# A NaN-skipping row maximum on one core: some write-backs of tile 1 and tile 5 are given to VectorE

## The chip, the cores and the metric

The kernel runs on one core of a Trainium2 chip. The core's engines have their own instruction streams and wait for each other through semaphores: VectorE (DVE in the profile), ScalarE (ACT), GpSimd (POOL), TensorE (PE, unused here) and SyncE (SP), which issues the transfers. The metric is the device time of one launch in microseconds (us).

## What is computed

```python
def setup_inputs():
    batch, seq, dim = 32, 2048, 2048
    x = np.random.randn(batch, seq, dim).astype(np.float32)
    mask = np.random.rand(batch, seq, dim) < 0.1
    x[mask] = np.nan
    return {"x": x, "axis": -1}

def reference(x: np.ndarray, axis: int) -> np.ndarray:
    return np.nanmax(x, axis=axis).astype(np.float32)
```

Each of 65,536 rows of 2,048 numbers is reduced to its largest number that is not NaN. The input has 512 MiB, the output 256 KiB.

## The kernel before

The rows are dealt out over 128 partitions, 512 rows to each. The unit of the program is the **quarter row**: 512 elements per partition. The table `TILES` lists 74 tiles, and each entry has three lists in quarter rows: how the tile is loaded, in which pieces it is worked on, and in which parts it is reduced. The first tile has 4 quarter rows, all others 28 (7 rows per partition). Up to the 58th tile nearly all read `([28], [7, 9, 12], [16, 12])`: one load, three pieces, two reductions. Every eighth one (tiles 9, 17, 25, 33, 41) reads `([28], [9, 12, -7], [8, 20])`. From tile 59 on the pieces and then also the loads get smaller, up to 17 pieces and 19 loads in the last.

The work on a tile:

1. SP issues its loads into one of three buffers `xt` (line 245). A load waits for the last reduction of the tile that had the buffer before, three tiles ago.
2. ACT makes the **keys** of a piece (lines 419 to 427): from the upper 16 bits of each float it computes, with a Prelu of two slopes, a 16-bit number in one of three buffers `kt` of 12 quarter rows. For an ordinary number the key only mirrors these bits; for a NaN the slope sends it to a value that stands for minus infinity.
3. The **write-back** turns the keys round again (times -1, plus `TOP`) and puts them over the upper halves of the floats in `xt`, every second 16-bit word. By the sign of the piece in the table it is POOL (a positive number, `tensor_scalar`, line 279) or ACT (a negative one, `activation` with Copy, lines 392 to 404). A floating number regulates when it is issued: a negative one is held back until the next piece's keys, a positive one is joined to the piece ahead.
4. DVE takes the maximum along the rows (`tensor_reduce`, line 286).

At the end a row that held only NaNs is marked, and the results are stored.

Each engine executes its instructions in the order in which this loop issues them. The class `Order` puts one semaphore wait on each for what it needs: a key for its load and for a free key buffer, a write-back for its key, a reduction for the write-backs under it. The last piece of a tile that opens a new key buffer also waits until the next key buffer is free (lines 416 to 418); in the tiles of 7, 9 and 12 that buffer is the first piece's own, so that the third key of a tile waits for the first write-back of the same tile. `joints` finds pairs of a POOL and an ACT write-back that one reduction needs together, and `last` keeps for each key buffer the last event of each writer. The lines of the profile are those of this file; almost all of ACT's instructions have line 269, POOL's 279 and DVE's 286, which are the helpers that record them.

Of the kernel before, what the change touches and what calls it, by code (L numbers as in the profile page):

```python
# [10 lines left out]
Q = D // 4  # L11
# [2 lines left out]


TILES = (
    [([4], [4], [4])]
    + [([28], [7, 9, 12], [16, 12])] * 7
    + [([28], [9, 12, -7], [8, 20])]
    + [([28], [7, 9, 12], [16, 12])] * 7  # L20
    + [([28], [9, 12, -7], [8, 20])]
# [50 lines left out]
TOP = 0x7F7F  # L72
# [6 lines left out]


def total(pieces):
    return sum(sum(map(abs, p)) if isinstance(p, tuple) else abs(p) for p in pieces)


def with_last(c):

    return isinstance(c, float) and c > 0


def joints(pieces, reds):  # L90

    flat = []
    at = 0
    for step, parts in enumerate(pieces):
        for c in parts if isinstance(parts, tuple) else (parts,):  # L100

            if with_last(c):
                flat[-1] = (flat[-1][0], at + abs(c), False, step)
            else:
                flat.append((at, at + abs(c), c < 0, step + isinstance(c, float)))
            at += abs(c)
    needs = []
    done = 0
    for n in reds:
        over = [i for i, (a, b, _, _) in enumerate(flat) if a < done + n and b > done]  # L110
        done += n
        pools = [i for i in over if not flat[i][2]]
        backs = [i for i in over if flat[i][2]]
        if pools and backs and flat[pools[-1]][3] > flat[backs[-1]][3]:
            backs = []
        needs.append(pools[-1:] + backs[-1:])
    pairs = {}
    for need in needs:
        if len(need) == 2 and all(sum(i in n for n in needs) == 1 for i in need):
            for i in need:  # L120
                pairs[i] = tuple(need)
    return pairs
# [61 lines left out]
def kernel(  # L184
# [15 lines left out]
    nc = tc.nc  # L200
    P = nc.NUM_PARTITIONS
    f32, i32 = mybir.dt.float32, mybir.dt.int32
    i16, u16 = mybir.dt.int16, mybir.dt.uint16
    ALU = mybir.AluOpType
    ACT = mybir.ActivationFunctionType
# [34 lines left out]
    def load(out, source, deps):  # L240
        nonlocal turn
        e = order.add(
            "sp",
            nc.sync,
            lambda: nc.sync.dma_start(out=out, in_=source),  # L245
            deps + lanes[turn],
            lane=f"load{turn}",
            step=16,
        )
        lanes[turn] = [e]  # L250
        turn = (turn + 1) % LANES
        return e
# [12 lines left out]
    def act(deps, pair=None, **kw):  # L265
        return order.add(
            "act",
            nc.scalar,
            lambda: nc.scalar.activation(**kw),  # L269
            deps,  # L270
            lane=pair,
            joint=pair is not None,
        )

    def pool(deps, pair=None, **kw):
        return order.add(
            "pool",
            nc.gpsimd,
            lambda: nc.gpsimd.tensor_scalar(**kw),  # L279
            deps,  # L280
            lane=pair,
            joint=pair is not None,
        )

    def dve(deps, do, **kw):
        return order.add("dve", nc.vector, lambda: do(**kw), deps)  # L286
# [36 lines left out]
    clock = 0  # L323

    def last(uses):

        return list({back: e for back, _, e in sorted(uses, key=lambda u: u[1])}.values())

    key = 0
# [6 lines left out]
    for gi, (s, g) in enumerate(zip(rows, GROUPS)):  # L336
# [8 lines left out]
        for loads, pieces, reds in g:  # L345
            assert sum(loads) == total(pieces) == sum(reds)
            xt, before = xts[number % BUFS], free[number % BUFS]
            number += 1
            landed = []
            at = 0  # L350
            for c in loads:
                c *= Q
                if ahead:
                    e = ahead.pop(0)
                else:
                    e = load(xt[:, at : at + c], xg[:, base + at : base + at + c], before)
# [4 lines left out]
            at = done = 0  # L361
# [7 lines left out]
            flat = [c for c in each if not with_last(c)]  # L369
# [3 lines left out]
            piece = 0  # L373

            def cleaned(a, b, k, i, e):

                nonlocal clock
                clock += 1
                both = [(a, b, k, flat[i] < 0, clock)]
                if i in pairs:  # L380
                    if pairs[i] not in half:
                        half[pairs[i]] = both
                        return
                    both += half.pop(pairs[i])
                for a, b, k, back, when in both:
                    kfree[k].append((back, when, e))
                    clean.append((a, b, e))
# [17 lines left out]

            for parts in pieces:
                parts = parts if isinstance(parts, tuple) else (parts,)
                c = int(sum(map(abs, parts))) * Q
                here = [l for a, b, l in landed if a < at + c and b > at]
                kold = []  # L410
                if used + c > KEYS:
                    key = (key + 1) % NKEYS
                    used = 0
                    kold, kfree[key] = last(kfree[key]), []
                    assert all(k != key for q in half.values() for _, _, k, _, _ in q)
                    if at + c == sum(loads) * Q and number not in ALONE:

                        kold = kold + last(kfree[(key + 1) % NKEYS])
                e_key = act(
                    here + kold,  # L420
                    out=kts[key][:, used : used + c],
                    in_=xt[:, at : at + c].bitcast(i16)[:, 1::2],
                    func=ACT.Prelu,
                    bias=EDGE,
                    scale=-1.0,
                    alpha=float(TOP - LOW) / (EDGE - NAN),
                )
                release()
                for c in parts:
                    on = more.pop(0)  # L430
                    back, wait, c = c < 0, isinstance(c, float), int(abs(c)) * Q
                    kp = kts[key][:, used : used + c]
                    used += c
                    at += c
                    if back:
                        held.append((at - c, at, key, kp, e_key, piece))
                        if not wait or at == sum(loads) * Q:
                            release()
                    else:
                        group.append((at - c, used - c, key))  # L440
                        if not on:
                            assert all(k == key for _, _, k in group)
                            lo, klo, _ = group[0]
                            e = pool(
                                [e_key],
                                name(piece),
                                out=xt[:, lo:at].bitcast(i16)[:, 1::2],
                                in0=kts[key][:, klo:used],
                                scalar1=-1.0,
                                scalar2=float(TOP),  # L450
                                op0=ALU.mult,
                                op1=ALU.add,
                            )
                            group = []
                            cleaned(lo, at, key, piece, e)
                    piece += not on
                    open_ = [h[0] for h in held + group] + [p[0] for q in half.values() for p in q]
                    while reds and done + reds[0] <= min([at] + open_):
                        n = reds.pop(0)


                        lo = done - 1 if done % D else done
                        done += n
                        row = (base + lo) // D
                        if done % D:
                            m, to = 1, xt[:, done - 1 : done].bitcast(f32)
                        else:
                            m = max(n // D, 1)
                            to = acc[:, row : row + m]
                        e = dve(  # L470
                            [e for a, b, e in clean if b > lo and a < done] + part,
                            nc.vector.tensor_reduce,
                            out=to,
                            in_=xt[:, lo:done]
                            .bitcast(f32)
                            .rearrange("p (c d) -> p c d", c=m),
                            axis=mybir.AxisListType.X,
                            op=ALU.max,
                        )
                        part = [e] if done % D else []  # L480
                        after.append(e)
# [10 lines left out]
        else:  # L492
            e = find(after, maxima(lo, flagged))
            ready += [e] * (gi + 1 - len(ready))
        if gi == len(GROUPS) - 1:
            e = find_late(late_after, late_acc, late)
            ready[LATE] = e
    for (og, bits), e in zip(stores, ready):
# [6 lines left out]
            step=16,  # L505
# [38 lines left out]
```

## Time and profile before

| | before |
|---|---|
| time, median of 3 runs (lowest to highest) | 1250.2 us (1250.16 to 1250.34) |
| time of the profiled execution | 1250.19 us |
| its span | 1248.9 us |
| DVE busy, instructions | 1110.2 us, 183 |
| ACT busy, instructions | 974.4 us, 290 |
| POOL busy, instructions | 1162.3 us, 243 |
| read from memory | 536.87 MB, 430 GB/s over the span |

The profile is of one execution, and its span is 1.3 us shorter than that execution's time. A group's row gives the line, the engine, the operation, output and input with their shapes and the count, then the time it was busy, the mean of one in ns, and the engine's idle time just before these instructions with what ended it. A timeline's row gives start and length in us (of several instructions in a run, with their count), and in brackets the idle time ahead and what released it. A row of the windows gives the stretch, its length, the busy time of DVE, ACT and POOL with counts, the granted TensorE clock, and the share and rate of the transfers.

### The profile page before, as it was taken

Reading aid. Unit: us, or ns where it says so; the run is one execution under the profiler, and the core shown is the slowest. Engines: PE = TensorE matmul, PEld = TensorE weight load, DVE = VectorE, ACT = ScalarE, POOL = GpSimd, SP = SyncE. Lnnn points to the kernel's source line nnn. Section 1 sums busy time; section 2 is a strip of 40 time slices with the busy share of each in tenths; the row PEclk is TensorE's granted clock in tenths of the full one; section 3 lists DMA queues with packets and bytes.
Section 4 is the critical chain, followed back from the end, with each engine's and each line's share of the span. In section 5 each row is a group of like instructions: output and inputs, shape, how many; then the busy total and the mean of one; then the engine's idle time right before and its main releaser. Section 6 shows DMA issues by size and latency. Waiting matters only on the chain.

```text
span 1248.9 us, 918 instructions
## 1 busy us (share of the span) xinstructions
DVE 1110.2 (89%) x183; ACT 974.4 (78%) x290; POOL 1162.3 (93%) x243
## 2 busy tenths in 40 slices
DVE  0888989888889888898988888988888998999999
ACT  3777887778777877788777877777777789989998
POOL 2999989998999899998999899999999989999898
DMA  9999999999999999999999999999999999999998
GB/s 416 439 415 439 441 441 426 426 441 441 433 419 441 441 433 421 439 441 439 430 424 441 439 435 419 441 441 433 422 437 441 437 434 419 437 428 431 433 426 327
DMA packets 17720, 537.21 MB, mean 430 GB/s; under 512 B 2736, under 2 KB 2736, under 8 KB 5552
## 3 DMA queue, kind: packets, MB, share of 16 engines
q1 hardware_dynamic: 17712, 537.14, 99.6%
q14 instruction: 8, 0.07, 0.0%
HBM read 536.87 MB, written 0.26 MB: 430 GB/s over the span
## 4 chain that ended last, share of the span: by engine, by line
DVE 37%; DMA 36%; POOL 16%; ACT 9%; issue 2%; SPq 0%
DMA xt<-in_x_dram 36%; DVE acc L286 23%; POOL xt L279 16%; DVE lead L286 14%; ACT kt L269 8%; ACT xt L269 1%; SPq L245 0%; SPq L263 0%; SPq L254 0%
## 5 line engine op out<-in xcount | busy, mean ns | idle before, releaser
L279 POOL TENSOR_SCALAR xt<-kt 128x6144 int16<-128x6144 uint16 (+9 forms) x237 | 1161.1, 4899 | 83.2 <-ACT kt L269 69.4
L269 ACT ACTIVATE kt<-xt 128x6144 uint16<-128x6144 int16 (+11 forms) x256 | 914.1, 3610 | 266.3 <-DMA xt<-in_x_dram 245.6
L286 DVE TENSOR_REDUCE acc<-xt 128x3 f32<-128x6144 f32 (+4 forms) x123 | 896.3, 7329 | 129.8 <-POOL xt L279 122.5
L286 DVE TENSOR_REDUCE lead<-xt 128x1 f32<-128x2048 f32 (+3 forms) x57 | 213.2, 3812 | 4.0 <-POOL xt L279 3.9
L269 ACT ACTIVATE xt<-kt 128x512 int16<-128x512 uint16 (+4 forms) x32 | 61.8, 1932 | 0.7
L269 ACT ACT_TABLE_LOAD x1 | 1.3, 1283 | 3.3 <-PEq L263 3.3
L318 DVE MEMSET lead<- 128x1 f32 x1 | 0.1, 59 | 3.4 <-PEq L263 3.4
L279 POOL TENSOR_SCALAR lead<-lead 128x91 int32<-128x91 f32 x1 | 0.6, 552 | 0.1
L286 DVE SCALAR_TENSOR_TENSOR acc<-acc 128x414 f32<-128x414 f32 x1 | 0.6, 592 | 0.0
L314 POOL TENSOR_TENSOR lead<-lead 128x91 int32<-128x91 int32 x1 | 0.4, 377 | 0.1
L525 POOL MEMSET const-float32-0.0<- 128x1 f32 x1 | 0.1, 99 | 0.2 <-issue 0.2
L269 ACT ACTIVATE lead<-lead 128x1 f32<-128x1 f32 x1 | 0.2, 203 | 0.0
L286 DVE SCALAR_TENSOR_TENSOR lead<-lead 128x7 f32<-128x7 f32 x1 | 0.2, 167 | 0.0
L525 POOL MEMSET const-bfloat16-1.0<- 128x1 bf16 x1 | 0.1, 102 | 0.0
L525 POOL MEMSET const-uint8-127<- 128x1 uint8 x1 | 0.1, 102 | 0.0
L525 POOL MEMSET const-float32-1.0<- 128x1 f32 x1 | 0.1, 99 | 0.0
## 6 DMA issues: line engine op xcount, KB each, us to landing
xt<-in_x_dram SPq DMA_DIRECT2D x61, 7168.0 KB, 22.6
xt<-in_x_dram SPq DMA_DIRECT2D x3, 4096.0 KB, 18.1
xt<-in_x_dram SPq DMA_DIRECT2D x5, 2048.0 KB, 30.6
xt<-in_x_dram SPq DMA_DIRECT2D x3, 3072.0 KB, 25.0
xt<-in_x_dram SPq DMA_DIRECT2D x8, 1024.0 KB, 29.1
xt<-in_x_dram SPq DMA_DIRECT2D x3, 2560.0 KB, 22.4
xt<-in_x_dram SPq DMA_DIRECT2D x2, 3584.0 KB, 23.3
xt<-in_x_dram SPq DMA_DIRECT2D x3, 2304.0 KB, 26.2
```

The lines of the kernel that those rows point to most:

```text
L269: lambda: nc.scalar.activation(**kw),
L279: lambda: nc.gpsimd.tensor_scalar(**kw),
L286: return order.add("dve", nc.vector, lambda: do(**kw), deps)
L314: lambda: nc.gpsimd.tensor_tensor(out=bits, in0=bits, in1=none, op=ALU.add),
L318: e_warm = order.add("dve", nc.vector, lambda: nc.vector.memset(warm, 1.0), [])
L525: nc = _bacc.Bacc("TRN2", target_bir_lowering=False, num_devices=1)
```

## The change

In the table the one piece of tile 1 becomes `4j`, and the first piece of tile 5 becomes `7j`. A new function `backer` tells the writer of a piece from its number: complex is DVE, negative ACT, anything else POOL. It takes the place of the test `c < 0` in `joints`, in `cleaned` and in the loop over the pieces. The loop gets a branch in which DVE does the write-back with `tensor_scalar`, in its own stream at the place where the loop issues it.

```diff
+    [([4], [4j], [4])]
+    + [([28], [7, 9, 12], [16, 12])] * 3
+    + [([28], [7j, 9, 12], [16, 12])]
+    + [([28], [7, 9, 12], [16, 12])] * 3
...
+POOL, ACT, DVE = range(3)
+
+
+def backer(c):
+
+    return DVE if isinstance(c, complex) else ACT if c < 0 else POOL
...
-        pools = [i for i in over if not flat[i][2]]
-        backs = [i for i in over if flat[i][2]]
+        pools = [i for i in over if flat[i][2] == POOL]
+        backs = [i for i in over if flat[i][2] == ACT]
...
-                both = [(a, b, k, flat[i] < 0, clock)]
+                both = [(a, b, k, backer(flat[i]), clock)]
...
-                    back, wait, c = c < 0, isinstance(c, float), int(abs(c)) * Q
+                    by, wait, c = backer(c), isinstance(c, float), int(abs(c)) * Q
...
-                    if back:
+                    if by == DVE:
+                        e = dve(
+                            [e_key],
+                            nc.vector.tensor_scalar,
+                            out=xt[:, at - c : at].bitcast(i16)[:, 1::2],
+                            in0=kp,
+                            scalar1=-1.0,
+                            scalar2=float(TOP),
+                            op0=ALU.mult,
+                            op1=ALU.add,
+                        )
+                        cleaned(at - c, at, key, piece, e)
+                    elif by == ACT:
                         held.append((at - c, at, key, kp, e_key, piece))
```

The names `POOL`, `ACT` and `DVE` are numbers at the top of the file. Inside the kernel function, line 204 before the change and unchanged by it, stands `ACT = mybir.ActivationFunctionType`. The new test `by == ACT` is in that function, while `backer` and `joints` are outside it. What does not pass the first two tests goes to the last branch, which is POOL's.

What this makes of the instructions is seen in their order. First DVE around tile 5 (its data are in `xt1`), after the change; a wait named `SP_sequencer_49` or `SP_49` is one that the listing does not resolve to the waited engine by name:

```order
L296 TENSOR_REDUCE acc<-xt0 128x4 [waits order_pool]
L296 TENSOR_REDUCE acc<-xt0 128x3 [waits order_pool]
L296 TENSOR_SCALAR xt1<-kt1 128x3584 [waits SP_49]
L296 TENSOR_REDUCE acc<-xt1 128x4 [waits SP_sequencer_49,order_pool]
L296 TENSOR_REDUCE acc<-xt1 128x3 [waits order_pool]
```

The write-back stands behind both reductions of tile 4 (`xt0`). On ACT, the keys of tile 5 and of tile 6 (`xt2`), after the change:

```order
L279 ACTIVATE kt1<-xt1 128x3584 [waits order_load4]
L279 ACTIVATE kt2<-xt1 128x4608 [waits order_pool]
L279 ACTIVATE kt0<-xt1 128x6144 [waits SP_sequencer_49]
L279 ACTIVATE kt1<-xt2 128x3584 [waits order_load5]
L279 ACTIVATE kt2<-xt2 128x4608 [waits order_pool]
```

The third key of tile 5 no longer waits for POOL; the wait on its row is the one for DVE's write-back of `kt1`.

Second, ACT at tile 9 (`xt2`), before the change:

```order
L269 ACTIVATE kt1<-xt2 128x4608 [waits order_load8]
L269 ACTIVATE kt2<-xt2 128x6144 [waits order_pool]
L269 ACTIVATE kt0<-xt2 128x3584 [waits order_pool]
L269 ACTIVATE xt2<-kt0 128x3584 [waits SP_49]
L269 ACTIVATE kt1<-xt0 128x3584 [waits order_load9]
```

and after it:

```order
L279 ACTIVATE kt1<-xt2 128x4608 [waits order_load8]
L279 ACTIVATE kt2<-xt2 128x6144 [waits order_pool]
L279 ACTIVATE kt0<-xt2 128x3584 [waits order_pool]
L279 ACTIVATE kt1<-xt0 128x3584 [waits order_load9]
L279 ACTIVATE kt2<-xt0 128x4608 [waits order_pair9_1]
```

ACT's write-back of the 3584 elements is gone. It is on POOL, here after the change, from tile 9 to tile 10 (`xt0`):

```order
L289 TENSOR_SCALAR xt2<-kt1 128x4608 [waits SP_49]
L289 TENSOR_SCALAR xt2<-kt2 128x6144 [waits SP_49]
L289 TENSOR_SCALAR xt2<-kt0 128x3584 [waits SP_49]
L289 TENSOR_SCALAR xt0<-kt1 128x3584 [waits SP_49]
L289 TENSOR_SCALAR xt0<-kt2 128x4608 [waits SP_49]
```

The third row is new there. Third, the end of the program, where the last tile (`xt1`) has pieces of one and two quarter rows. ACT's last rows before the change:

```order
L269 ACTIVATE kt0<-xt1 128x1024 [waits order_load10]
L269 ACTIVATE xt1<-kt0 128x512 [waits SP_49]
L269 ACTIVATE kt0<-xt1 128x1024 [waits order_load11,order_load12]
L269 ACTIVATE kt0<-xt1 128x1024 [waits order_load13,order_load0]
L269 ACTIVATE kt0<-xt1 128x512 [waits order_load1]
L269 ACTIVATE xt1<-kt0 128x512 [waits SP_49]
L269 ACTIVATE kt0<-xt1 128x1024 [waits order_load2,order_load3]
L269 ACTIVATE kt0<-xt1 128x512 [waits order_load4]
L269 ACTIVATE xt1<-kt0 128x512 [waits SP_49]
```

and POOL's last rows after it:

```order
L289 TENSOR_SCALAR xt1<-kt2 128x512 [waits SP_49]
L289 TENSOR_SCALAR xt1<-kt0 128x512 [waits SP_49] x2
L289 TENSOR_SCALAR xt1<-kt0 128x1024 [waits SP_49] x2
L289 TENSOR_SCALAR xt1<-kt0 128x512 [waits SP_49]
L289 TENSOR_SCALAR xt1<-kt0 128x512
L289 TENSOR_SCALAR xt1<-kt0 128x512 [waits SP_49]
L289 TENSOR_SCALAR xt1<-kt0 128x1024 [waits SP_49]
L289 TENSOR_SCALAR xt1<-kt0 128x512 [waits SP_49]
```

In the whole listing ACT has 32 write-backs (`xt<-kt`) before the change and none after it. POOL has 237 write-backs before it and 267 after it: 32 more, and the two that are now DVE's fewer.

More of the change, by code (lines that the diff above doesn't have):

```diff
@@ L16 @@
 TILES = (
-    [([4], [4], [4])]
-    + [([28], [7, 9, 12], [16, 12])] * 7
+    [([4], [4j], [4])]
+    + [([28], [7, 9, 12], [16, 12])] * 3
+    + [([28], [7j, 9, 12], [16, 12])]
+    + [([28], [7, 9, 12], [16, 12])] * 3
     + [([28], [9, 12, -7], [8, 20])]
@@ L81, in total @@
 def total(pieces):
-    return sum(sum(map(abs, p)) if isinstance(p, tuple) else abs(p) for p in pieces)
+    return sum(int(abs(c)) for p in pieces for c in (p if isinstance(p, tuple) else (p,)))
 def with_last(c):
     return isinstance(c, float) and c > 0
+POOL, ACT, DVE = range(3)
+def backer(c):
+    return DVE if isinstance(c, complex) else ACT if c < 0 else POOL
 def joints(pieces, reds):
@@ L102, in joints @@
             if with_last(c):
-                flat[-1] = (flat[-1][0], at + abs(c), False, step)
+                flat[-1] = (flat[-1][0], at + int(abs(c)), POOL, step)
             else:
-                flat.append((at, at + abs(c), c < 0, step + isinstance(c, float)))
-            at += abs(c)
+                flat.append((at, at + int(abs(c)), backer(c), step + isinstance(c, float)))
+            at += int(abs(c))
     needs = []
@@ L407 @@
                 parts = parts if isinstance(parts, tuple) else (parts,)
-                c = int(sum(map(abs, parts))) * Q
+                c = total((parts,)) * Q
                 here = [l for a, b, l in landed if a < at + c and b > at]
```

## Prediction

> Tiles are numbered from 1 in processing order, quarter rows are counted as in the table. K is a key instruction on ScalarE (ACT), W a write-back, R a reduction on VectorE (DVE); K1, W2, R2 count within a tile.
>
> **What bounds the kernel now.** The page first: busy shares, rate per slice, the load queue.
>
> ```profile
> span 1248.9 us, 918 instructions
> DVE 1110.2 (89%) x183; ACT 974.4 (78%) x290; POOL 1162.3 (93%) x243
> GB/s 416 439 415 439 441 441 426 426 441 441 433 419 441 441 433 421 439 441 439 430 424 441 439 435 419 441 441 433 422 437 441 437 434 419 437 428 431 433 426 327
> q1 hardware_dynamic: 17712, 537.14, 99.6%
> L269 ACT ACTIVATE xt<-kt 128x512 int16<-128x512 uint16 (+4 forms) x32 | 61.8, 1932 | 0.7
> ```
>
> The load queue is occupied 99.6% of the span and GpSimd (POOL) 93%: two candidates. The timeline decides. Here are tiles 4 to 8, and tile 58 far behind:
>
> ```profile
> 69.41 15.15 DVE L286 TENSOR_REDUCE acc<-xt 128x4 f32<-128x8192 f32 x2 [1.80 <-POOL xt L279]
> 73.44 7.12 ACT L269 ACTIVATE kt<-xt 128x3584 uint16<-128x3584 int16 x2 [4.12 <-DMA xt<-in_x_dram]
> 76.71 33.61 POOL L279 TENSOR_SCALAR xt<-kt 128x3584 int16<-128x3584 uint16 x6 [0.21 <-ACT kt L269]
> 80.95 5.32 ACT L269 ACTIVATE kt<-xt 128x6144 uint16<-128x6144 int16 x1 [0.39 <-POOL xt L279]
> 86.37 15.15 DVE L286 TENSOR_REDUCE acc<-xt 128x4 f32<-128x8192 f32 x2 [1.81 <-POOL xt L279]
> 90.32 7.12 ACT L269 ACTIVATE kt<-xt 128x3584 uint16<-128x3584 int16 x2 [4.04 <-DMA xt<-in_x_dram]
> 103.24 15.15 DVE L286 TENSOR_REDUCE acc<-xt 128x4 f32<-128x8192 f32 x2 [1.72 <-POOL xt L279]
> 107.24 7.12 ACT L269 ACTIVATE kt<-xt 128x3584 uint16<-128x3584 int16 x2 [4.10 <-DMA xt<-in_x_dram]
> 120.17 15.15 DVE L286 TENSOR_REDUCE acc<-xt 128x4 f32<-128x8192 f32 x2 [1.78 <-POOL xt L279]
> 124.19 7.12 ACT L269 ACTIVATE kt<-xt 128x3584 uint16<-128x3584 int16 x2 [4.12 <-DMA xt<-in_x_dram]
> 970.37 12.40 ACT L269 ACTIVATE kt<-xt 128x3584 uint16<-128x3584 int16 x3 [4.33 <-DMA xt<-in_x_dram]
> ```
>
> ACT waits some 4 us per tile for a landing, so landings set the pace: (970.37 - 73.44) / 53 = 16.92 us per tile. POOL follows with almost nothing to spare, as its durations show:
>
> ```profile
> L279 POOL TENSOR_SCALAR xt<-kt 128x6144 int16<-128x6144 uint16 x61 | 429.6, 7043 | 5.2 <-ACT kt L269 0.5
> L279 POOL TENSOR_SCALAR xt<-kt 128x4608 int16<-128x4608 uint16 x52 | 277.7, 5340 | 8.8 <-ACT kt L269 5.1
> L279 POOL TENSOR_SCALAR xt<-kt 128x3584 int16<-128x3584 uint16 x51 | 214.1, 4199 | 45.9 <-ACT kt L269 44.7
> L269 ACT ACTIVATE xt<-kt 128x3584 int16<-128x3584 uint16 x6 | 25.2, 4204 | 0.2
> L286 DVE TENSOR_REDUCE acc<-xt 128x3 f32<-128x6144 f32 x52 | 340.3, 6544 | 4.7 <-POOL xt L279 4.7
> L286 DVE TENSOR_REDUCE acc<-xt 128x1 f32<-128x2048 f32 x3 | 6.8, 2279 | 6.8 <-POOL xt L279 6.8
> ```
>
> 7.04 + 5.34 + 4.20 = 16.58, and the six in 33.61 us above leave 0.08 to 0.09 between two: 16.82 per tile. So up to tile 58 the loads bound and POOL is 0.1 us per tile below them. From tile 59 (990.97) small pieces make POOL dearer, and ACT takes over a share:
>
> ```profile
> 990.97:1244.85 253.88, 249.90 (x66) 237.34 (x110) 234.63 (x71) 1.00 0.99 424
> L279 POOL TENSOR_SCALAR xt<-kt 128x1024 int16<-128x1024 uint16 (+11 forms) x70 | 234.6, 3352 | 19.7 <-ACT kt L269 15.5
> L269 ACT ACTIVATE xt<-kt 128x2048 int16<-128x2048 uint16 x6 | 14.9, 2486 | 0.1
> L269 ACT ACTIVATE xt<-kt 128x1024 int16<-128x1024 uint16 x7 | 9.4, 1340 | 0.1
> L269 ACT ACTIVATE xt<-kt 128x512 int16<-128x512 uint16 x11 | 8.5, 769 | 0.2
> L269 ACT ACTIVATE xt<-kt 128x3584 int16<-128x3584 uint16 x1 | 4.2, 4213 | 0.0
> L269 ACT ACTIVATE xt<-kt 128x1536 int16<-128x1536 uint16 x2 | 3.8, 1922 | 0.1
> ```
>
> In these 253.9 us DVE is busy 249.9, ACT 237.3, POOL 234.6: nobody has 40 us over.
>
> **The part the few words leave out.** The test `by == ACT` stands in the function where ACT means the activation types, not the number 1, so it is never true. The order shows it: all 32 write-backs of ACT (five in tiles 9, 17, 25, 33 and 41, 27 from tile 59) are gone from ACT and stand on POOL. This is the largest term.
>
> **The tail, from tile 59.** ACT's 27 write-backs there took 14.9 + 9.4 + 8.5 + 4.2 + 3.8 = 40.8 us. On POOL they cost the same: 3584 elements take 4.20 on either engine. POOL then has 234.6 + 40.8 = 275.4 us in 97 instructions, with 97 x 0.08 = 7.8 between them: 283.2 us where there were 253.8. DVE's 250 and what is left to ACT, 237 - 41 = 196, fit beside it, and the loads need 16 x 16.92 = 270.7. POOL becomes the bound of the tail, +29.4 us. The end behind it stays:
>
> ```profile
> 1234.67 10.09 POOL L279 TENSOR_SCALAR xt<-kt 128x1024 int16<-128x1024 uint16 x8 [0.15 <-ACT kt L269]
> 1233.97 13.24 DVE L286 TENSOR_REDUCE lead<-xt 128x1 f32<-128x2048 f32 x6
> ```
>
> POOL's last write-back ends at 1244.76, the span 4.1 later: one reduction, the mark, the store.
>
> **Tile 5.** POOL loses W1 (4.20), but that buys nothing, since POOL then waits. DVE executes W1 behind R2 of tile 4, so from 69.41 + 15.15 = 84.56. No row shows this operation on DVE; DVE's rows grow by (6.544 - 2.279) / 4096 = 1.04 ns per element, which gives 3.9 us for 3584, W1 done at 88.5 (before: 80.91). K3 now waits for it (the order shows the wait), with tile 6's keys queued behind: K3 88.5 to 93.9 (before 86.3). W2 is done at 86, POOL idles until W3, 93.9 to 101.0 (before 93.5): every later write-back is 7.45 late. R1 of tile 5 runs 88.5 to 97.2, R2 101.0 to 107.5, then the buffer is free for tile 8's load.
>
> How much of that reaches the loads? A load on an empty queue costs more than its 16.92:
>
> ```profile
> xt<-in_x_dram SPq DMA_DIRECT2D x1, 1024.0 KB, 4.8
> 67.64 22.66 DMA xt<-in_x_dram
> ```
>
> The first, 1024 KB, took 4.8 us, its share of the pace is 16.92 / 7 = 2.4, so 2.4 is fixed. A tile lands at the later of issue + 2.4 + 16.92 and the landing before + 16.92. Now issue to landing is 22.66, so 22.66 - 19.32 = 3.3 us of lateness are free. A tile with ACT's 7 is special:
>
> ```profile
> 141.11 9.26 ACT L269 ACTIVATE kt<-xt 128x4608 uint16<-128x4608 int16 x2 [4.08 <-DMA xt<-in_x_dram]
> 158.06 10.82 DVE L286 TENSOR_REDUCE acc<-xt 128x5 f32<-128x10240 f32 x1 [1.47 <-ACT xt L269]
> 191.87 7.13 ACT L269 ACTIVATE kt<-xt 128x3584 uint16<-128x3584 int16 x2 [4.14 <-DMA xt<-in_x_dram]
> ```
>
> Its R2 needs W7, which ACT made beside POOL's W12; now it follows W12 on POOL, 4.2 later. With POOL at 16.82 per tile from 101.0 on (tile 9: 151.5 to 168.2), and the loss as time by which a tile lands later than before (tile 11 loses what tile 10 did):
>
> | tile | R2 ends, before | now | frees the load of | lands, before | now | loss |
> |---|---|---|---|---|---|---|
> | 5 | 101.5 | 107.5 | 8 | 124.2 | 126.8 | 2.6 |
> | 6 | 118.4 | 125.9 | 9 | 141.1 | 145.2 | 4.1 |
> | 7 | 135.3 | 142.8 | 10 | 158.0 | 162.1 | 4.1 |
> | 9 | 168.9 | 168.2 + 10.8 = 179.1 | 12 | 191.85 | 198.4 | 6.5 |
>
> Tile 12's K1 is then done at 198.4 + 3.2 = 201.6 and POOL free of tile 11 at 168.2 + 2 x 16.82 = 201.9: the loads bound again. In tiles 17, 25, 33 and 41 R2 ends 4.15 + 16.74 + 10.82 = 31.7 after the landing; with 19.3 that is 51.0 against 3 x 16.92 = 50.8, so 0.2 each, 0.8. Tile 59 starts 7.3 late. Bounds: without the fixed 2.4 only POOL's own lateness counts: 101.04 + 53 x 16.82 = 992.5, 1.5 late; if every free us proves unusable, 7.45 + 4.2 = 11.6.
>
> [...]
>
> **Tile 1.** W and R move from POOL to DVE, about equal in cost; its buffer is wanted by the fourth load, behind two tiles still in flight until 39.5. Nothing.
>
> **Sum.** 990.97 + 7.3 + 283.2 + 4.1 = 1285.6, 1 us for POOL's waits for keys in the tail (ACT has slack), so a span of 1286.6. The profiled execution took 1250.19 for its span of 1248.9, 1.3 more, and agrees with the median 1250.2. Forecast **1288 us**.
>
> **Rivals.**
> (a) The tail's waits stay. POOL idled 19.7 us there; if these come on top instead of being filled: 234.6 + 19.7 + 40.8 + 27 x 0.08 = 297.3, and 1288 + 13 = 1301. For: a piece's key can still be late. Against: loads and keys have 13 and 87 us to spare, so POOL should have a backlog.
> (b) ACT keeps its write-backs, as the few words say. Then POOL recovers in tile 9, and the loss ends at 4.1: 1254. The order speaks against it.
> (c) Not slower. POOL's write-backs run faster once ACT writes nothing beside them into the same tile. To hold 1250, the tail's 275.4 us must shrink to 253.8 - 7.8 - 7.3 = 238.7, by 13%. Against: 3584 takes 4199 ns on POOL whether ACT writes back or, as in most tiles, does not.
>
> **How the numbers follow.** Forecast 0.85, (a) 0.10, (b) 0.03, (c) 0.02. Bounds of the first: 1288 - 5.8 - 1 = 1281, and 1288 + 4.3 + some of (a); range 1280 to 1299. A measurement tells 0.2%, 2.5 us, from no change: (b) is slower too, so slower 0.97, the same 0.02, faster 0.01.
>
> **What would show it.** No write-back of ACT; POOL with some 266 write-backs, busy 1162.3 + 61.8 - 2.5 - 4.2 = 1217; a POOL gap of 7 to 8 us in tile 5 behind a late K3; landings 2 to 8 us late from tile 8 on; POOL without gaps from tile 59. I am wrong if ACT still writes back, if POOL has long gaps in the tail, or if DVE's W1 is far from 88.5.

## The result, and the profile after

The changed kernel took **1289.95 us** (median of 4 runs, 1288.51 to 1290.77) against 1250.18 us (1250.16 to 1250.34): 39.8 us more, ratio 1.0316 with a 95% interval of 1.0304 to 1.0329. The forecast was 1288. The page of the changed kernel, busy shares, then the rate in each slice, the load queue, and the groups of POOL and ACT with count, busy time, mean and the idle time ahead:

```profile
span 1288.7 us, 919 instructions
DVE 1117.4 (87%) x185; ACT 914.5 (71%) x258; POOL 1216.0 (94%) x273
GB/s 403 456 427 376 431 413 433 428 427 427 431 441 431 434 425 429 427 436 425 443 431 427 400 449 431 431 427 438 441 431 427 433 433 430 436 428 431 428 377 3
q1 hardware_dynamic: 17712, 537.14, 96.9%
L289 POOL TENSOR_SCALAR xt<-kt 128x6144 int16<-128x6144 uint16 (+8 forms) x267 | 1214.8, 4550 | 69.4 <-ACT kt L279 51.1
L279 ACT ACTIVATE kt<-xt 128x6144 uint16<-128x6144 int16 (+11 forms) x256 | 913.0, 3609 | 347.0 <-DMA xt<-in_x_dram 250.9
```

No group of ACT writes `xt` any more; POOL has 267 write-backs and 53.7 us more busy time (1216.0 - 1162.3). The load queue, occupied 99.6% before, is at 96.9% of a longer span, and the last slice moves 3 GB/s: the loads are done some 30 us before the end, and POOL works off what lies in the buffers. The share of POOL's busy time hardly rose (93 to 94%), but from tile 59 on its gaps are gone. The timeline of POOL from tile 58's last pieces on:

```profile
989.25 12.46 POOL L289 TENSOR_SCALAR xt<-kt 128x5120 int16<-128x5120 uint16 x2 [0.17 <-ACT kt L279]
1002.23 43.98 POOL L289 TENSOR_SCALAR xt<-kt 128x4096 int16<-128x4096 uint16 x10 [0.53 <-ACT kt L279]
1046.62 238.08 POOL L289 TENSOR_SCALAR xt<-kt 128x4096 int16<-128x4096 uint16 x87 [0.41 <-ACT kt L279]
1284.78 0.55 POOL L289 TENSOR_SCALAR lead<-lead 128x91 int32<-128x91 f32 x1
```

97 write-backs from 1002.23 to 1284.70, with one wait of 0.41 us among them. (A row joins instructions with only short gaps between them, some 0.08 us here.) Tile 59 starts 1002.23 - 990.97 = 11.3 us later than before, the tail lasts 282.5 us where it had 253.8, and 4.0 us remain to the span's end: 11.3 + 28.7 - 0.1 = 39.9, the whole difference of the spans (39.8).

The other half of the story is tile 5. Rows from the timelines of the changed kernel there, of all engines (rows between them are left out):

```profile
73.27 7.12 ACT L279 ACTIVATE kt<-xt 128x3584 uint16<-128x3584 int16 x2 [4.11 <-DMA xt<-in_x_dram]
80.47 5.31 POOL L289 TENSOR_SCALAR xt<-kt 128x4608 int16<-128x4608 uint16 x1 [4.13 <-ACT kt L279]
84.32 3.48 DVE L296 TENSOR_SCALAR xt<-kt 128x3584 int16<-128x3584 uint16 x1
87.83 12.34 ACT L279 ACTIVATE kt<-xt 128x6144 uint16<-128x6144 int16 x3 [7.45 <-DVE xt L296]
93.24 107.92 POOL L289 TENSOR_SCALAR xt<-kt 128x6144 int16<-128x6144 uint16 x19 [7.46 <-ACT kt L279]
100.33 6.55 DVE L296 TENSOR_REDUCE acc<-xt 128x3 f32<-128x6144 f32 x1 [3.73 <-POOL xt L289]
106.91 0.33 SPq L255 DMA_DIRECT2D xt<-in_x_dram  x1
127.04 7.12 ACT L279 ACTIVATE kt<-xt 128x3584 uint16<-128x3584 int16 x2 [0.34 <-DMA xt<-in_x_dram]
146.69 9.26 ACT L279 ACTIVATE kt<-xt 128x4608 uint16<-128x4608 int16 x2 [3.19 <-DMA xt<-in_x_dram]
198.38 7.12 ACT L279 ACTIVATE kt<-xt 128x3584 uint16<-128x3584 int16 x2 [4.41 <-DMA xt<-in_x_dram]
```

One reads it from top to bottom: ACT has two keys ready at 80.4 and then waits 7.45 us for DVE's write-back; POOL is idle for 7.46 us; the load of tile 8 is issued at 106.91, when the second reduction of tile 5 has ended, and lands at 127.0 instead of 124.2. Tile 9 is ready at 146.69 instead of 141.11, tile 12 at 198.38 instead of 191.87.

### The profile page after: what moved, and what is told of

Same layout as the page of the kernel before. It is cut to its first block, busy times and chain, and to the rows that moved or that the text cites. A ratio compares the mean times of both kernels' runs of the same rounds, so it can differ in the third digit from the quotient of the medians.

```text
span 1288.7 us, 919 instructions
## 1 busy us (share of the span) xinstructions
DVE 1117.4 (87%) x185; ACT 914.5 (71%) x258; POOL 1216.0 (94%) x273
## 3 DMA queue, kind: packets, MB, share of 16 engines
q1 hardware_dynamic: 17712, 537.14, 96.9%
## 4 chain that ended last, share of the span: by engine, by line
POOL 41%; DMA 30%; DVE 20%; ACT 7%; issue 1%; SPq 0%; ACTq 0%
POOL xt L289 41%; DMA xt<-in_x_dram 30%; DVE acc L296 20%; ACT kt L279 7%; DVE xt L296 0%; DVE lead L296 0%; SPq L273 0%; ACTq L179 0%; SPq L264 0%
## 5 line engine op out<-in xcount | busy, mean ns | idle before, releaser
L289 POOL TENSOR_SCALAR xt<-kt 128x6144 int16<-128x6144 uint16 (+8 forms) x267 | 1214.8, 4550 | 69.4 <-ACT kt L279 51.1
L296 DVE TENSOR_REDUCE lead<-xt 128x1 f32<-128x2048 f32 (+3 forms) x57 | 215.9, 3817 | 29.6 <-POOL xt L289 29.5
L296 DVE TENSOR_SCALAR xt<-kt 128x2048 int16<-128x2048 uint16 (+1 forms) x2 | 4.8, 2396 | 4.1 <-ACT kt L279 4.1
## 6 DMA issues: line engine op xcount, KB each, us to landing
xt<-in_x_dram SPq DMA_DIRECT2D x61, 7168.0 KB, 22.6
```

## The experiments

Each was compared with the kernel before on the same chip (1250.5 us in all of them). "Names apart" is the changed kernel with the three numbers renamed, so that the test is true for ACT's pieces. (The line that gives ACT its other meaning inside the function is 205 in the kernel before.) The diffs of the other experiments stand against this one or against the table of before; `...` marks what is left out.

```diff
-POOL, ACT, DVE = range(3)
+BY_POOL, BY_ACT, BY_DVE = range(3)
...
-                    elif by == ACT:
+                    elif by == BY_ACT:
```

**1. Names apart**, tiles 1 and 5 on DVE, all else as before.

> The changed kernel with the three numbers under names of their own, so that ACT keeps its 32 write-backs; tiles 1 and 5 on DVE. Theory (almost all of the loss is ACT's write-backs on POOL; tile 5 alone costs what the landings of tiles 9 and 10 showed after the change, 5.6 us): 1250.2 + 5.6 = 1255.8 us, tile 59 starting on POOL near 996.6. Rival (the DVE write-backs themselves carry the loss, whoever does the others): above 1275.

Measured 1255.89 us (1255.66 to 1256.04), ratio 1.0043 (1.0028 to 1.0058). Rows of POOL from its timeline:

```profile
80.64 5.31 POOL L289 TENSOR_SCALAR xt<-kt 128x4608 int16<-128x4608 uint16 x1 [4.11 <-ACT kt L279]
93.40 69.98 POOL L289 TENSOR_SCALAR xt<-kt 128x6144 int16<-128x6144 uint16 x12 [7.46 <-ACT kt L279]
166.84 33.53 POOL L289 TENSOR_SCALAR xt<-kt 128x3584 int16<-128x3584 uint16 x6 [3.46 <-ACT kt L279]
995.96 14.46 POOL L289 TENSOR_SCALAR xt<-kt 128x4096 int16<-128x4096 uint16 x3 [0.52 <-ACT kt L279]
```

The gap of 7.46 us in tile 5 is the same, but after tile 9, where ACT took the seven, POOL waits again (3.46): it has caught up with the landings, which are late themselves (tile 9 at 145.40 against 141.11). Tile 59 starts 5.0 us late (995.96 against 990.97), and in this execution the span ends 5.8 us later (1254.7 against 1248.9). So what the title names costs 5.4 us, as the theory expected, and the other 34 of the 39.8 hang on the name.

**2. All write-backs of ACT on POOL**, tiles 1 and 5 as before (the table of before with the code of the change).

> The table of before, tiles 1 and 5 on POOL, but with the test that is never true, so that POOL does all write-backs. Theory: the tail of 282.5 us in place of 253.8, and some 1.2 us for each of five tiles with a held-back seven: 1250.2 + 28.7 + 6 = 1285 us. Rival (POOL has room, since it is the stall in tile 5 that it never recovers from): below 1262.

Measured 1286.81 us (1285.11 to 1288.71), ratio 1.0291 (1.0276 to 1.0306): 36.3 us more, 1.8 above the theory. POOL has no room for this work, with or without the stall in tile 5.

**3. and 4. The same, split** at tile 59: the table of before, the names apart, and ACT keeps its write-backs either ahead of tile 59

```diff
-                    elif by == BY_ACT:
+                    elif by == BY_ACT and number < 59:
```

or, in the other, from it on (`number >= 59`).

> The table of before; ACT does its write-backs up to tile 58, POOL all from tile 59 on. Theory: POOL starts tile 59 at 991 as before and needs 282.5 us without a gap, then 4.0 to the end and 1.3 around: 1279 us. Rival (the stalls for keys add to it): 1290 and more, with over 10 us of idle time on POOL in the tail.

Measured 1279.16 us (1278.92 to 1279.24), ratio 1.0229 (1.0214 to 1.0244). POOL's timeline:

```profile
991.38 43.96 POOL L289 TENSOR_SCALAR xt<-kt 128x4096 int16<-128x4096 uint16 x10 [0.50 <-ACT kt L279]
1035.75 238.19 POOL L289 TENSOR_SCALAR xt<-kt 128x4096 int16<-128x4096 uint16 x87 [0.41 <-ACT kt L279]
1274.02 0.55 POOL L289 TENSOR_SCALAR lead<-lead 128x91 int32<-128x91 f32 x1
```

It starts 0.4 us later than before and runs 282.6 us with one wait of 0.41: the tail alone costs 28.7 us, and its waits for keys vanished into POOL's backlog.

> The table of before; POOL does the sevens of tiles 9, 17, 25, 33 and 41, ACT keeps all from tile 59 on. Theory: each makes the reduction under it 4.2 us late, the load of three tiles later meets an empty queue and lands 20.1 us after its issue, some 1.2 us later: 1250.2 + 5 x 1.2 = 1256 us. Rival (the prediction's own 2.4 us for an empty queue, 0.2 us a tile): 1251.2.

Measured 1257.49 us (1255.19 to 1259.02), ratio 1.0057 (1.0040 to 1.0074): 7.0 us for five pieces whose work POOL can do within the pace of 16.92 us per tile. Both expectations lie below the median: the theory's 1256 still among the runs, the rival's 1251.2 below all of them. The runs spread by 3.8 us, those of the kernel before by 0.1 beside them. How the loss comes about is seen at tile 17 of that kernel, in rows of ACT and of the load's issue:

```profile
278.41 9.26 ACT L279 ACTIVATE kt<-xt 128x4608 uint16<-128x4608 int16 x2 [4.09 <-DMA xt<-in_x_dram]
295.29 3.19 ACT L279 ACTIVATE kt<-xt 128x3584 uint16<-128x3584 int16 x1 [4.20 <-DMA xt<-in_x_dram]
310.13 0.33 SPq L255 DMA_DIRECT2D xt<-in_x_dram  x1
312.20 7.12 ACT L279 ACTIVATE kt<-xt 128x3584 uint16<-128x3584 int16 x2 [3.32 <-DMA xt<-in_x_dram]
329.83 7.12 ACT L279 ACTIVATE kt<-xt 128x3584 uint16<-128x3584 int16 x2 [4.13 <-DMA xt<-in_x_dram]
```

The keys that wait for a landing start 16.9 us apart, then 17.63: the load of tile 20 was issued only when the late reduction of tile 17 had freed its buffer, 310.13 - 278.41 = 31.7 us after the first key of tile 17 (27.8 before). The gap at this place was 18.81, 17.63, 17.84, 18.64 and 17.44 us for the five tiles, 5.8 us over five times 16.92. This execution, 1256.35 us, is near the lower end of the runs.

**5. Two pieces of tile 5 on DVE.** What does DVE's write-back cost, and why 3.48 us? Names apart, and:

```diff
-    + [([28], [7j, 9, 12], [16, 12])]
+    + [([28], [7j, 9j, 12], [16, 12])]
```

> Names apart, and in tile 5 both the piece of 7 and that of 9 on DVE, so that POOL has nothing to do when DVE begins. Theory (the write-back on DVE is fast, 1.3 us for 2048 and 2.0 for 3584 elements, and took 3.48 only because it began under a running write-back of POOL and did not move until that ended): the first takes 2.0 us, the second about 2.6, the third key starts 1.5 us earlier than in names_apart, 1253 us. Rival (the write-back on DVE takes about 1 ns per element whatever POOL does): 3.5 and 4.5 us, the third key starts at the same 87.8, and 1256 us or more.

Measured 1254.56 us (1253.80 to 1255.05), ratio 1.0031 (1.0019 to 1.0044). DVE's write-backs there, by form, and the timeline:

```profile
L296 DVE TENSOR_SCALAR xt<-kt 128x4608 int16<-128x4608 uint16 x1 | 2.7, 2727 | 0.0
L296 DVE TENSOR_SCALAR xt<-kt 128x3584 int16<-128x3584 uint16 x1 | 2.2, 2160 | 0.0
L296 DVE TENSOR_SCALAR xt<-kt 128x2048 int16<-128x2048 uint16 x1 | 1.3, 1311 | 4.4 <-ACT kt L279 4.4
```

```profile
84.59 4.79 DVE L296 TENSOR_SCALAR xt<-kt 128x3584 int16<-128x3584 uint16 x2
86.78 12.34 ACT L279 ACTIVATE kt<-xt 128x6144 uint16<-128x6144 int16 x3 [6.12 <-DVE xt L296]
```

With POOL idle (for 15.57 us, up to 92.19) the same 3584 elements took 2.16 us, and 4608 took 2.73. On the price the theory holds and its rival falls. The time is between the two forecasts, as is the start of the third key: 86.78 against 88.00 with the names apart, 1.2 us earlier and not 1.5.

**6. The write-back first.** The second reduction of tile 4 is held back until DVE's write-back of tile 5 is issued:

```diff
+    later = []
...
                         cleaned(at - c, at, key, piece, e)
+                        while later:
+                            later.pop()()
...
+                        if number == 4 and not reds:
+
+                            def reduce_later(needs=needs, what=what):
+                                free[3 % BUFS] = [dve(needs, nc.vector.tensor_reduce, **what)]
+
+                            later.append(reduce_later)
+                            continue
...
```

(`needs` and `what` are the waits and the operands that the reduction had before.)

> Names apart, tiles 1 and 5 on DVE, with DVE's write-back of tile 5 put ahead of the second reduction of tile 4 in DVE's stream. Theory (the 5.6 us come from the place behind that reduction): the write-back begins near 78, takes 2.0 us since POOL is idle there, the third key is as early as before, the reduction of tile 4 ends 2 us late, which is free: 1250.2 to 1250.7 us. Rival (DVE has no room for 2.0 us more, or the wait moves to tile 4's buffer): 1252 to 1256.

Measured 1250.83 us (1250.73 to 1250.95, 11 runs), ratio 1.0003 (0.9994 to 1.0012). Rows from the timeline:

```profile
78.06 2.18 DVE L296 TENSOR_SCALAR xt<-kt 128x3584 int16<-128x3584 uint16 x1
80.13 21.59 DVE L296 TENSOR_REDUCE acc<-xt 128x3 f32<-128x6144 f32 x3
80.68 12.47 POOL L289 TENSOR_SCALAR xt<-kt 128x4608 int16<-128x4608 uint16 x2 [4.13 <-ACT kt L279]
93.62 16.73 POOL L289 TENSOR_SCALAR xt<-kt 128x3584 int16<-128x3584 uint16 x3 [0.47 <-ACT kt L279]
```

The same instruction, one place earlier: POOL's gap of 7.46 is gone, and so is the loss (1250.83 lies within the runs of the kernel before, 1250.15 to 1250.95). It was the place in DVE's queue, not the work. At the earlier place the write-back waits for no second reduction, and it meets an idle POOL: 2.18 us and not 3.48.

**7. Tile 1 alone on DVE.**

> Names apart, only tile 1 on DVE. Theory: its buffer is free 1.4 us earlier, for a load that has two others ahead of it; no change, 1250.2 to 1250.6 us. Rival (an earlier start gains or an early stall costs): off by over 0.5 us either way.

Measured 1250.52 us (1250.29 to 1251.01, 11 runs), ratio 1.0001 (0.9992 to 1.0010): no difference.

**8. An attempt at a gain.** Names apart, and the table of before with the last two pieces on DVE:

```diff
-..., 2, 2, (1, -1.0), 1, 2, -1], [4, 4, 4, 4, 4, 4, 4])]
+..., 2, 2, (1, -1.0), 1, 2j, 1j], [4, 4, 4, 4, 4, 4, 4])]
```

> Names apart, the table of before, but the last two pieces of the last tile (2 and 1 quarter rows) on DVE in place of POOL and ACT. Theory (DVE's write-back costs half of POOL's and DVE is idle ahead of its last reduction): that reduction starts some 0.3 us earlier, 1249.9 to 1250.1 us, the only place found where DVE's write-back could gain. Rival (it waits for POOL's write-back running beside it): 1250.4 or more.

Measured 1251.56 us (1251.46 to 1251.80, 11 runs), ratio 1.0009 (1.0000 to 1.0018). Slower by 1.1 (every run is above every run of the kernel before). The theory was wrong, and so was the rival's reason: POOL's last write-back had ended at 1243.66, ahead of DVE's two. DVE's timeline here, and then in the kernel before:

```profile
1229.85 15.44 DVE L296 TENSOR_REDUCE lead<-xt 128x1 f32<-128x2048 f32 x7
1245.20 1.05 DVE L296 TENSOR_SCALAR xt<-kt 128x1024 int16<-128x1024 uint16 x2
1246.29 2.29 DVE L296 TENSOR_REDUCE lead<-xt 128x1 f32<-128x2048 f32 x1
```

```profile
1231.78 15.43 DVE L286 TENSOR_REDUCE lead<-xt 128x1 f32<-128x2048 f32 x7
1247.25 0.17 DVE L286 SCALAR_TENSOR_TENSOR lead<-lead 128x7 f32<-128x7 f32 x1
```

In the kernel before the reductions follow each other without a gap to the end: DVE is the bound there, and POOL's write-back lies beside it. On DVE the two write-backs stand in that row, and their 1.05 us come to about the loss. What looked like idle time in the chain of waits ("issue", 1.5 us ahead of the last reduction) was the reduction before. No version was found that is faster than the kernel before.

## Why the prediction was right, point by point

- **"The part the few words leave out"** is shown: names apart 5.4 us, all of ACT's write-backs on POOL 36.3, both 39.8. The parts alone (5.4, 7.0, 28.7) sum to 41.1. The 1.3 too much are less than the 3.8 by which the runs with the sevens spread, so nothing can be read from them.
- **The tail** was forecast at 283.2 us with 1 us of waits on top. It took 282.5, and 282.6 on its own. No such 1 us was seen. POOL's 97 write-backs were busy 274.5 and not 275.4. Rival (a), the waits for keys added on top, is refuted: of 19.7 us of idle time only 8.5 are left in this stretch. They are almost all gaps between instructions: ACT is named for 0.9, of which 0.53 lie ahead of tile 59.

```profile
L289 POOL TENSOR_SCALAR xt<-kt 128x2048 int16<-128x2048 uint16 (+10 forms) x97 | 274.5, 2829 | 8.5 <-ACT kt L279 0.9
```

- **Rival (b)** failed on its condition; run by itself, its 1254 compares with the 1255.9 of names apart, so its loss of 4.1 was 1.3 too small. **Rival (c)**, faster write-backs on POOL without ACT beside them, is refuted by the same row: 274.5 us where 275.4 were summed from the rows of before, 0.3% less and not 13%.
- **Tile 5**: the way was right (W1 behind R2 of tile 4, the third key behind W1, POOL idle, the load late), and experiment 6 shows that the place alone does it. W1 was forecast done at 88.5 and was at 87.8. That this came near is luck, for the reason was wrong: 1.04 ns per element, taken from the reductions, make 3.9 us, and with POOL idle it took 2.16 (experiment 5) and 2.18 us (experiment 6), and the 2048 elements of tile 1 took 1.31. It took 3.48 where a write-back of POOL was running when it began: POOL's ended at 80.47 + 5.31 = 85.78, DVE's at 87.80, 2.02 later, close to the 2.16 that it takes with POOL idle. That it did not move until POOL's had ended is an estimate from these times.
- **Where a term was mis-sized**: "2.4 is fixed" for a load on an emptied queue, and with it "0.2 each" for the later sevens and "Tile 59 starts 7.3 late". The load of tile 8, issued at 106.91, landed 20.1 us later and not 19.3. The load of tile 9 took 21.5, so that tile 9 came 5.6 us late where 4.1 were forecast:

```profile
125.15 0.33 SPq L255 DMA_DIRECT2D xt<-in_x_dram  x1
xt<-in_x_dram SPq DMA_DIRECT2D x1, 7168.0 KB, 21.5
```

  At tile 12 the forecast fits again, 198.38 against 198.4, by luck: its load was issued 0.7 us earlier than forecast (178.42 against 179.1) and took about as much longer. Then tiles 17, 25, 33 and 41 cost (981.62 - 198.38) - (970.37 - 191.87) = 4.7 us in place of 0.8, by the keys of tile 58 and of tile 12 in both kernels:

```profile
981.62 12.40 ACT L279 ACTIVATE kt<-xt 128x3584 uint16<-128x3584 int16 x3 [4.04 <-DMA xt<-in_x_dram]
```

  With 11.3 for 7.3 and no waits in the tail for the 1 us assumed, the forecast of 1288 becomes 1291, above the measured 1290 by the 0.7 us that the tail took less. So the forecast came within 2 us partly because these errors have opposite signs. The sign "landings 2 to 8 us late" held up to tile 12 (2.9 to 6.5) and no longer at tile 58 (11.25).
- **Tile 1** was costed at nothing; 1250.52 against 1250.48.

## What to carry to other kernels

A change is what its instruction order says, not what its description says: here one name that meant something else inside the function moved 32 instructions to another engine, and counting each engine's instructions before and after found it. POOL, 93% busy and 0.1 us per tile below the pace, had little room. In the tail it got 39.9 us of work more; 11 of them filled its waits, and the other 28.7 made the tail longer. A fast instruction at a late place in DVE's stream cost what stood ahead of it: 2.2 us of work began at 84.32 and not at 78.06 as in experiment 6, and held the third key back by 7.45. The stall was hidden only in part. The buffer of tile 5 came free 5.4 us late (106.88 against 101.52) and the load into it landed 2.9 us late, 20.1 us after its issue in place of 22.6, so 2.5 were hidden. What was not hidden was not won back: names apart started tile 59 5.0 us late, behind landings at a pace of 16.92 us.

## What the runs showed of the hardware that was not expected

A load issued when the queue was nearly empty did not have one price in these runs. At tile 9, where ACT's work was on POOL, the load of tile 12 was issued at 172.94 in the kernel of experiment 4 and at 172.78 in that of experiment 2, both some 2.0 us before the first key of tile 11 started on the load ahead. The key of tile 12 started at 193.79 and 192.65: 20.85 and 19.87 us. At tile 17 it was 329.83 - 310.13 = 19.70 and 330.73 - 309.44 = 21.29, and tile 20 landed 17.63 and 19.25 us after tile 19, 0.7 and 2.3 above the pace. Two programs that are alike up to that point differ as well: the load of tile 9 took 21.5 us after the change and 20.1 with the names apart (145.40 - 125.30, from the end of the reduction that frees its buffer). The kernels in which POOL does the sevens spread by 2.3 to 3.8 us from run to run, the one that moved only the tail by 0.3. But names apart, where the buffer of tile 5 came free as late (107.03, and 106.88 after the change), spread by only 0.4, so a late load alone does not explain the spread. Why the same situation costs 0.7 us once and 2.3 another time stays open.
